# Padding tiles in SBUF so that matmul operands begin at other byte offsets, in a two-block network on one core

## The chip, the core and the metric

The kernel runs on one core of a Trainium2 chip. The metric is device time in microseconds (us) from one execution of the whole program. The profile used below was taken in one execution; other runs were timed without it.

TensorE (PE in the profile) multiplies a **stationary** operand, which a weight load (PEld) puts into the array, by a **moving** operand, which streams past it column by column. In the code `pe.matmul(ps, lhsT=..., rhs=...)` names them: `lhsT` is stationary, `rhs` is moving. The profile prints a matmul as `out<-moving,stationary`. Both operands are read from SBUF, where every tile has a byte offset that is the same in all 128 partitions.

## What is computed

The reference chains two small networks on one sequence of 256 tokens with width 1024, all in float32. Cut to what matters:

```python
# first block
a = rmsnorm(h, sb_pre_g)
q, k, v = split(a @ sb_w_qkv)
h = h + rmsnorm(merge(stick_breaking_attention(q, k, v)) @ sb_w_o, sb_post_g)
h = h + rmsnorm(conv_ffn(rmsnorm(h, ffn_pre_g[0]), ...), ffn_post_g[0])
# second layer: keys, values and forget gates from one projection, queries from another
k, v, f = split(rmsnorm(h, kv_norm_g) @ w_kvf)
q = rmsnorm(h, fox_pre_g) @ fox_w_q
h = h + rmsnorm(merge(forgetting_attention(q, k, v, cumsum(log_sigmoid(f + b_f)))) @ fox_w_o, fox_post_g)
h = h + rmsnorm(conv_ffn(rmsnorm(h, ffn_pre_g[1]), ...), ffn_post_g[1])
# second block
x = pool_layer(h, ...)      # u, z = h @ w_in; window means of u, grouped product, times silu(z), @ w_out
x = mla_layer(x, ...)       # latent q and kv, rotary part, causal softmax, times silu(z), @ w_out
return rmsnorm(x, final_norm)

def conv_ffn(x, w_up, conv_w, conv_b, w_down):      # w_up [1024, 5632], w_down [2816, 1024]
    gate, up = split(causal_depthwise_conv3(x @ w_up, conv_w) + conv_b)
    return (gelu(gate) * up) @ w_down
```

## The kernel before

**Arithmetic.** Each float32 operand is held as a high part and a low part in the type fp32r, and each product is made of three matmuls: high by high, high by low, low by high. The helper `mm3` (L70 to L72) issues them one after the other, and `mm3s` (L78, L79, L81) does it for several blocks of the contraction at once. So nearly every matmul of the program stands at one of these six lines, and it is the tile names that tell the stages apart.

**Weights.** All weights come from HBM once. The SyncE queue loads 1 MB chunks into three `raw` buffers. ScalarE (ACT) copies a part of 1024 elements per partition into a tile `wh` (L55), and VectorE (DVE) subtracts to get `wl` (L59). There are eight `wh` and eight `wl` buffers. This work is issued in between the other work of ACT and DVE by calls of `bg`.

**Two orientations of matmul.** Where the output is wanted transposed (features on partitions), the weights are stationary and the activations move: 256 columns, one for each token. This is `proj_A`, which makes `psu` (the up-projections of both FFN layers, and the input projection of the pool layer), `psq`, `psz` and `psg`. Where the output is wanted with tokens on partitions, the activations are stationary and 512 columns of weights move. This is `out_rows`, which makes `accD` (down-projection, from `gT`: tiles `gh`, `gl`), `accO` (attention outputs, from `oT` or `yT`) and `accP` (pool output, from `yT`), and `values_all`, which makes `accV`. Every matmul is preceded by a weight load of its own, of 128 columns.

**Placement.** Tiles are placed in SBUF in the order in which their pools are opened: `cst`, `rawp`, `whp`, `wlp`, `gp`, `nat`, `jk`, `sm`, `atp`, and then the pools of one stage (`sb` and `sbv`; `ff` and `fg`; `fx` and `fxv`; `pl` and `plc`; `ml` and `mlc`), which are closed at the stage's end. A tile's offset is thus the sum of what was placed ahead of it. Taken modulo 512 bytes, it comes to few values, because most tiles are multiples of 512 bytes long: in the kernel before all `wh` and `wl` buffers lie at 96, and all activations that meet weights (`aT`, `fT`, `qT`, `kT`, `ph`, `oT`, `gT`, `yT`) at 416. Steps inside these tiles (128, 256 or 512 columns of 4 bytes) are multiples of 512 bytes, but for the halves of the 192- and 320-column weight parts in the last layer, which are 256 bytes off.

**Order.** The order of instructions on each engine is the order of the code (`manual_schedule`), and semaphores are put in where tiles depend on each other.

Of the kernel before, what the change touches and what calls it, by code (L numbers as in the profile page):

```python
# [7 lines left out]
F32 = mybir.dt.float32  # L8
# [7 lines left out]
P = 128  # L16
# [11 lines left out]
TW = 1024  # L28
L3 = 384
WBUFS = 8  # L30
RAWB = 3
NLE_SET = 6

# [2 lines left out]
def tile_net(ctx: ExitStack, tc: tile.TileContext, t, out):  # L36
# [4 lines left out]
    cst = ctx.enter_context(tc.tile_pool(name="cst", bufs=1))  # L41
    rawp = ctx.enter_context(tc.tile_pool(name="rawp", bufs=RAWB))
    whp = ctx.enter_context(tc.tile_pool(name="whp", bufs=WBUFS))
    wlp = ctx.enter_context(tc.tile_pool(name="wlp", bufs=WBUFS))
    gp = ctx.enter_context(tc.tile_pool(name="gp", bufs=3))
    nat = ctx.enter_context(tc.tile_pool(name="nat", bufs=2))
    jk = ctx.enter_context(tc.tile_pool(name="jk", bufs=1))
    sm = ctx.enter_context(tc.tile_pool(name="sm", bufs=4))
    atp = ctx.enter_context(tc.tile_pool(name="atp", bufs=1))
    pacc = ctx.enter_context(tc.tile_pool(name="pacc", bufs=4, space=PSUM))  # L50
    pmm = ctx.enter_context(tc.tile_pool(name="pmm", bufs=4, space=PSUM))


    def hi_copy(hi, src, scale=1.0):
# [102 lines left out]
    def bg_hi():  # L157

        n = nxt["hi"]
        if n >= len(parts) or (n >= WBUFS and parts[n - WBUFS]["used"] < parts[n - WBUFS]["need"]):  # L160
            return False
# [11 lines left out]
    def bg_lo():  # L173
        while nxt["lo"] < nxt["hi"]:
# [4 lines left out]
            if n == specs[q["chunk"]][1][-1]:  # L179
                load_w(q["chunk"] + RAWB)  # L180

    def bg(m=1):
        for _ in range(m):
            bg_lo()
            if not bg_hi():
                break
        bg_lo()
# [116 lines left out]
    def gain(name, idx=None, g=None):  # L304
        src = t[name][idx] if idx is not None else t[name]
        n = src.shape[0]
        if g is None:
            g = gp.tile([P, D], F32, tag="g", name="g")[:, 0:n]
        nc.sync.dma_start(out=g, in_=src.unsqueeze(0).to_broadcast([P, n]))
        return g  # L310

    load_w(RAWB - 1)

# [298 lines left out]
    bg(0)  # L612
    with tc.tile_pool(name="sb", bufs=2) as sb, tc.tile_pool(name="sbv", bufs=1) as sbv:
        vv = [sbv.tile([P, NT, D], F32R, name=n) for n in ("vh", "vl")]
        oT = [sbv.tile([P, KD, S], F32R, name=n) for n in ("oTh", "oTl")]
        g_post = gain("sb_post_g", 0)
        values_all(aT, W["sb_v"], vv, {
# [101 lines left out]
    def ffn(l, aT, a1, late, dst):  # L719


        cp = conv[l]
        with tc.tile_pool(name=f"ff{l}", bufs=3) as ff, tc.tile_pool(name=f"fg{l}", bufs=1) as fg:
            gT = [fg.tile([P, NF, S], F32R, name=n) for n in ("gh", "gl")]

            def conv_gate(f, ps):
                y = ff.tile([P, 2, S], F32, tag="yc", name="yc")
                for u in range(2):
                    q = u * NF + f
                    act.activation(out=y[:, u, :], in_=ps[:, u * S:(u + 1) * S],  # L730
                                   func=AF.Identity, bias=cp[:, 132 + q:133 + q],
                                   scale=cp[:, 88 + q:89 + q])
                for u in range(2):
                    q = u * NF + f
                    for d in (1, 2):
                        w = cp[:, 88 - 44 * d + q:89 - 44 * d + q]
                        dve.scalar_tensor_tensor(out=y[:, u, d:S],  # L737
                                                 in0=ps[:, u * S:(u + 1) * S - d],
                                                 scalar=w, in1=y[:, u, d:S],
                                                 op0=ALU.mult, op1=ALU.add)  # L740
                    if u == 0:
                        act.activation(out=y[:, 0, :], in_=y[:, 0, :], func=AF.Gelu_apprx_tanh)  # L742
                bg_hi()
                dve.tensor_tensor(out=y[:, 1, :], in0=y[:, 0, :], in1=y[:, 1, :], op=ALU.mult)
                bg_lo()
                split(gT[0][:, f, :], gT[1][:, f, :], y[:, 1, :])
                bg(1)

            xs = nat_start(aT, [W["up_g", l, 0], W["up_u", l, 0]], lambda: all_T(a1, aT, 1))
            for c in range(1, NF // 2):  # L750
                wg, wu = get_w(W["up_g", l, c]), get_w(W["up_u", l, c])
                for pp in range(2):
                    f = 2 * c + pp
                    ps = mm_tile("psu")
                    proj_A(ps[:, 0:256], aT, wg, pp * P, KD)
                    proj_A(ps[:, 256:512], aT, wu, pp * P, KD)
                    conv_gate(f, ps)
                    if f == 10:
                        g_post, g = late()

            for e in range(2):
                ps = mm_tile("psn")
                nat_T(ps[:, 0:256], xs, e)
                nat_T(ps[:, 256:512], xs, e + 2)
                conv_gate(e, ps)
            acc = [acc_pair(f"accD{i}") for i in range(NT)]
            wd = {}
            for m, f in enumerate(DOWN):
                if f % 2 == 0:
                    wd[f // 2] = get_w(W["down", l, f // 2])  # L770
                for i in range(NT):
                    if m < NF - TAIL[i]:
                        out_rows(acc[i], i, gT, wd[f // 2], [(f, f % 2)], m == 0, False)
                if m < NF - TAIL[0]:
                    bg(1)
            tail = [[(f, f) for f in DOWN[NF - x:]] for x in TAIL]
            w = lambda f, c0, n: wd[f // 2](f % 2, c0, n)
            return edge(lambda: out_rows(acc[0], 0, gT, w, tail[0], False, True, by_half=True),
                        lambda: out_rows(acc[1], 1, gT, w, tail[1], False, True, by_half=True),
                        acc, lambda i, a: post_add(i, a, g_post), g, dst)  # L780


    def causal_mask(m):

        pool.memset(m, 0.0)
        pool.affine_select(out=m, in_=m, pattern=[[-1, S]], compare_op=ALU.is_ge, fill=NEG, base=P,
                           channel_multiplier=1)
# [39 lines left out]
    with tc.tile_pool(name="fxa", bufs=1) as fxa:  # L827
# [6 lines left out]
        table_set(NLE_SET)  # L834
        with tc.tile_pool(name="fx", bufs=2) as fx, tc.tile_pool(name="fxv", bufs=1) as fxv:
            vv = [fxv.tile([P, NT, D], F32R, name=n) for n in ("vh", "vl")]
            oT = [fxv.tile([P, KD, S], F32R, name=n) for n in ("oTh", "oTl")]
            bf = sm.tile([H, 1], F32, tag="bf", name="bf", bufs=1)
            nc.sync.dma_start(out=bf, in_=t["b_f"].rearrange("(h o) -> h o", o=1))
# [100 lines left out]
    with tc.tile_pool(name="pl", bufs=2) as pl_, tc.tile_pool(name="plc", bufs=1) as plc:  # L940
# [61 lines left out]
        def group(g):  # L1002
            wg = get_w(W["p_g", g])
            pT_, zs = st.pop(("pl", g)), st.pop(("zs", g))
            yT = [pl_.tile([P, 4, S], F32R, tag=n, name=n) for n in ("yh", "yl")]
            for c in range(2):
                ps = mm_tile("psg")
                for pp in range(2):
                    f = 2 * c + pp
                    proj_A(ps[:, pp * S:(pp + 1) * S], pT_, wg, f * P, 4)  # L1010
                for pp in range(2):
                    f = 2 * c + pp
                    y = zs[:, f, :]
                    q = 4 * g + f
                    dve.scalar_tensor_tensor(out=y, in0=ps[:, pp * S:(pp + 1) * S],
                                             scalar=pscale[:, q:q + 1], in1=y,
                                             op0=ALU.mult, op1=ALU.mult)
                    split(yT[0][:, f, :], yT[1][:, f, :], y)
                bg(3)
            st["y", g] = yT  # L1020
# [58 lines left out]
    with tc.tile_pool(name="ml", bufs=2) as ml, tc.tile_pool(name="mlc", bufs=1) as mlc:  # L1079
# [3 lines left out]
        gain("mla_q_norm_2", 0, gq)  # L1083
        gain("mla_kv_norm_2", 0, gkv)
        causal_mask(cmask)
        qT = [mlc.tile([P, 3, S], F32R, name=n) for n in ("qTh", "qTl")]
        kT = [mlc.tile([P, 2, S], F32R, name=n) for n in ("kTh", "kTl")]

# [127 lines left out]
        def values(g):  # L1216
            wkv = st.pop(("wkv", g))
            v = [ml.tile([P, NT, 512], F32R, tag=n, name=n, bufs=1) for n in ("vh", "vl")]
            for i in range(NT):
                psv = mm_tile("psv")  # L1220
                po = psv.rearrange("p (a b) -> p a b", a=4)
                for k in range(2):
                    r = [x.rearrange("p (a b) -> p a b", a=4)[:, :, 128:256] for x in wkv(k, 0, 1024)]
                    mm3(po, (kT[0][:, k, tok(i)], kT[1][:, k, tok(i)]), r, k == 0, k == 1)
                split(v[0][:, i, :], v[1][:, i, :], psv)
            bg(1)
            st["v", g] = v
            st["y", g] = [[ml.tile([P, 2, S], F32R, tag=f"{n}{a}", name=n, bufs=1) for n in ("yh", "yl")]
                          for a in range(2)]

# [253 lines left out]
```

## Time and profile before

| | us |
|---|---|
| three timed runs, median | 987.77 |
| lowest and highest of the three | 986.27 and 990.99 |
| the profiled execution, its own time | 987.21 |
| the profiled execution, span from first to last instruction | 985.5 |

The profile counts an engine as busy while at least one of its instructions runs. A matmul's recorded time is from its start to the end of its pass through the array, and the next one starts long before that: recorded times of 277 ns for 256 columns overlap. What a matmul costs in a dense stretch is the **step**, the time from its start to the start of the next matmul. It can be read from the starts in a timeline, or from the number of matmuls in a stretch.

### The profile page before, as it was taken

The numbers are of one execution on the slowest core, as the hardware profiler recorded it, in microseconds if no ns is written. First come the engines' busy times: TensorE is split into PE (matmuls) and PEld (weight loads), VectorE is DVE, ScalarE is ACT, GpSimd is POOL, SyncE is SP. The second block draws the span as 40 slices with busy tenths as digits, with TensorE's granted clock in tenths as the row PEclk, the third lists the DMA queues.
The fourth block names the chain that finished last, engine by engine and source line by source line (L and its number), as shares of the span: only waits on it lengthen the run. The fifth ranks groups of instructions, "written<-read, shape, count | busy, mean of one in ns | idle before, by whom it ended". The sixth has DMA issues, their size and how long they took to land.

```text
span 985.5 us, 17580 instructions
## 1 busy us (share of the span) xinstructions
PE 971.7 (99%) x6954; PEld 893.7 (91%) x6954; DVE 756.5 (77%) x1302; ACT 609.6 (62%) x1049; POOL 71.9 (7%) x181
## 2 busy tenths in 40 slices
PE   9999999999999999999999999999999999999997
PEld 6999789999887899889999988899998899999996
DVE  6577788999945979977999963776857677887776
ACT  6499866767634657657667653565434455766563
POOL 1022220000001000020000000200000020110100
PEclk9999999999999999999999999999999999999999
DMA  8733446575572754525666565375555344644421
GB/s 298 243 93 143 129 161 210 186 248 181 195 236 83 224 164 150 161 97 177 209 224 204 184 243 171 103 240 205 175 198 193 110 134 135 211 153 144 157 97 43
DMA packets 116164, 170.27 MB, mean 173 GB/s; under 512 B 4218, under 2 KB 93682, under 8 KB 116082
## 3 DMA queue, kind: packets, MB, share of 16 engines
q1 hardware_dynamic: 116002, 169.15, 52.0%
q8 instruction: 54, 0.88, 0.4%
q14 instruction: 28, 0.23, 0.1%
q0 software_dynamic: 64, 0.00, 0.0%
q10 hardware_dynamic: 16, 0.00, 0.0%
HBM read 168.10 MB, written 1.05 MB: 172 GB/s over the span
## 4 chain that ended last, share of the span: by engine, by line
PE 87%; ACT 4%; DVE 4%; POOL 1%; issue 1%; DMA 1%; POOLq 0%; DVEq 0%; ACTq 0%
PE psu L72 10%; PE psu L71 10%; PE psu L70 10%; PE accD L72 4%; PE accD L71 4%; PE accD L70 4%; PE psq L70 3%; PE psq L72 3%; PE psq L71 3%; PE accO L70 2%; PE accO L72 2%; PE accO L71 2%; DVE wl L59 2%; PE accP L70 2%; PE accP L72 2%; PE accP L71 2%
## 5 line engine op out<-in xcount | busy, mean ns | idle before, releaser
L59 DVE TENSOR_TENSOR wl<-raw,wh 128x1024 fp32r<-128x1024 f32 (+3 forms) x300 | 352.5, 1197 | 93.1 <-ACT wh L55 90.3
L55 ACT ACTIVATE wh<-raw 128x1024 fp32r<-128x1024 f32 (+3 forms) x316 | 315.3, 1026 | 83.3 <-PE accD L72 32.7
L70 PE MATMUL psu<-aT,wh 128*128 128x256 f32 x864 | 239.4, 277 | 0.6 <-ACT zs L950 0.6
L72 PE MATMUL psu<-aT,wl 128*128 128x256 f32 x864 | 239.4, 277 | 0.0
L71 PE MATMUL psu<-aT,wh 128*128 128x256 f32 x864 | 239.2, 277 | 0.0
L70 PEld LDWEIGHTS psu<-aT,wh 128*128 128x128 f32 x864 | 162.0, 188 | 0.9 <-ACT zs L950 0.8
L71 PEld LDWEIGHTS psu<-aT,wh 128*128 128x128 f32 x864 | 162.2, 188 | 0.0
L72 PEld LDWEIGHTS psu<-aT,wl 128*128 128x128 f32 x864 | 162.2, 188 | 0.0
L737 DVE SCALAR_TENSOR_TENSOR yc<-psu,conv,yc 128x255 f32<-128x255 f32 (+1 forms) x160 | 73.5, 480 | 11.2 <-ACT yc L730 8.1
L70 PE MATMUL accD<-wh,gh 128*128 128x512 f32 x176 | 69.6, 396 | 0.0
L71 PE MATMUL accD<-wl,gh 128*128 128x512 f32 x176 | 69.5, 395 | 0.0
L72 PE MATMUL accD<-wh,gl 128*128 128x512 f32 x176 | 69.5, 395 | 0.0
L337 POOL TENSOR_TENSOR ss<-ss,epsc 128x1 f32<-128x1 f32 x23 | 11.7, 507 | 616.3 <-ACT junk L374 616.2
L70 PE MATMUL psq<-aT,wh 128*128 128x256 f32 x192 | 54.1, 282 | 0.1
L72 PE MATMUL psq<-aT,wl 128*128 128x256 f32 x192 | 53.4, 278 | 0.0
L71 PE MATMUL psq<-aT,wh 128*128 128x256 f32 x192 | 53.4, 278 | 0.0
L730 ACT ACTIVATE yc<-psu,conv 128x256 f32<-128x256 f32 x80 | 40.8, 560 | 18.8 <-PE psu L72 18.7
L742 ACT ACTIVATE yc<-yc 128x256 f32<-128x256 f32 x44 | 18.4, 418 | 48.9 <-DVE yc L737 48.9
L71 PEld LDWEIGHTS accD<-wl,gh 128*128 128x128 f32 x176 | 33.0, 188 | 8.0
L72 PEld LDWEIGHTS accD<-wh,gl 128*128 128x128 f32 x176 | 33.0, 188 | 8.0
L70 PEld LDWEIGHTS accD<-wh,gh 128*128 128x128 f32 x176 | 33.0, 188 | 7.9
L55 ACT ACTIVATE qkh<-psq 128x512 fp32r<-128x512 f32 x32 | 19.0, 594 | 32.4 <-PE psq L72 32.2
(347 smaller groups left out, 2275.8 us busy)
## 6 DMA issues: line engine op xcount, KB each, us to landing
raw<-in_w_up_dram SPq DMA_DIRECT2D x44, 1024.0 KB, 5.1
raw<-in_w_down_dram SPq DMA_DIRECT2D x22, 1024.0 KB, 5.1
raw<-in_pool_w_in_dram SPq DMA_DIRECT2D x16, 1024.0 KB, 7.9
raw<-in_sb_w_qkv_dram SPq DMA_DIRECT2D x10, 1024.0 KB, 6.2
raw<-in_w_kvf_dram SPq DMA_DIRECT2D x8, 1024.0 KB, 5.8
raw<-in_pool_w_out_dram SPq DMA_DIRECT2D x8, 1024.0 KB, 5.2
raw<-in_mla_w_in_dram SPq DMA_DIRECT2D x8, 1024.0 KB, 6.0
raw<-in_mla_w_out_dram SPq DMA_DIRECT2D x8, 1024.0 KB, 6.4
```

The lines of the kernel that those rows point to most:

```text
L55: act.activation(out=hi, in_=src, func=AF.Copy, scale=scale)
L59: (eng or dve).tensor_tensor(out=lo, in0=src, in1=hi.bitcast(F32), op=ALU.subtract)
L70: pe.matmul(ps, lhsT=l[0], rhs=r[0], start=first, stop=False)
L71: pe.matmul(ps, lhsT=l[0], rhs=r[1], start=False, stop=False)
L72: pe.matmul(ps, lhsT=l[1], rhs=r[0], start=False, stop=last)
L337: pool.tensor_tensor(out=s0, in0=s0, in1=epsc[:, 0:1], op=ALU.add)
L730: act.activation(out=y[:, u, :], in_=ps[:, u * S:(u + 1) * S], func=AF.Identity, bias=cp[:, 132 + q:133 + q], scale=cp[:, 88 + q:89 + q])
L737: dve.scalar_tensor_tensor(out=y[:, u, d:S], in0=ps[:, u * S:(u + 1) * S - d], scalar=w, in1=y[:, u, d:S], op0=ALU.mult, op1=ALU.add)
L742: act.activation(out=y[:, 0, :], in_=y[:, 0, :], func=AF.Gelu_apprx_tanh)
```

## The change

A helper `pad` is added. It places a tile that nothing reads or writes. It is called for the pools `cst` (928 bytes) and `jk` (192 + 320 = 512 bytes), and in each stage ahead of the tiles that are stationary in 512-column matmuls (192 bytes), and in the last layer also ahead of `qT` and `kT` (320 bytes).

```diff
 WBUFS = 8
+APART = 320
 RAWB = 3
...
+    def pad(pl_, n, name):
+        pl_.tile([P, n // 4], F32, tag=name, name=name, bufs=1)
+
+    pad(cst, 928, "pad0")
+    pad(jk, 192 + APART, "pad1")
...
         vv = [sbv.tile([P, NT, D], F32R, name=n) for n in ("vh", "vl")]
+        pad(sbv, 512 - APART, "pad2")
         oT = [sbv.tile([P, KD, S], F32R, name=n) for n in ("oTh", "oTl")]
...
+            pad(fg, 512 - APART, "pad3")
             gT = [fg.tile([P, NF, S], F32R, name=n) for n in ("gh", "gl")]
...
             vv = [fxv.tile([P, NT, D], F32R, name=n) for n in ("vh", "vl")]
+            pad(fxv, 512 - APART, "pad4")
             oT = [fxv.tile([P, KD, S], F32R, name=n) for n in ("oTh", "oTl")]
...
+            if g == 0:
+                pad(pl_, 512 - APART, "pad5")
             yT = [pl_.tile([P, 4, S], F32R, tag=n, name=n) for n in ("yh", "yl")]
...
+        pad(mlc, APART, "pad7")
         qT = [mlc.tile([P, 3, S], F32R, name=n) for n in ("qTh", "qTl")]
...
+            if g == 0:
+                pad(ml, 512 - APART, "pad6")
             st["y", g] = [[ml.tile([P, 2, S], F32R, tag=f"{n}{a}", name=n, bufs=1) for n in ("yh", "yl")]
```

No instruction is added, removed or moved on any engine, and every wait stays. What changes is the byte offset of tiles. For the operands of the matmuls, modulo 512 bytes, as the built programs have it:

```
matmuls                                  moving            stationary
                                         before  after     before  after
psu psq psz psg   256 columns            416     320       96      0     activations past weights
accD accO accP    512 columns            96      0         416     0     weights past gT, oT, yT
accV psv          512 columns            96      0         416     320   weights past aT, kT
accS psr          256 columns            96      0         416     320   weights past aT, qT
accL              384, 320 columns       96      0         416     320   weights past aT
po (heads_out)    512, 256 columns       416     320       416     320   probabilities past values
po (last layer)   256, 128 columns       416     0         416     320   probabilities past values
z from ntri       384, 128 columns       416     320       416     0     log terms past a triangle, ones
z from qkh, qkl   256, 128 columns       416     320       416     320   keys, queries
transposes        128 columns            128     32        96, 416 0, 320
```

So in the kernel before every operand of a product of activations and weights begins 32 bytes past a multiple of 64, and afterwards at a multiple of 64. The distance from stationary to moving stays what it was, 320 or 192 modulo 512, except for `accD`, `accO`, `accP`, where it goes to 0, and for `z` from `ntri`, where it goes from 0 to 320. In the parts of the last layer that are 256 bytes off, both are shifted alike. The tiles that DVE, ACT and the DMA queues work on are shifted with them: `raw` from 96 to 0, `yc`, `us` and `zs` from 416 to 320.

## Prediction

> **What bounds the kernel now.** I first read the busy shares, the granted clock and the chain of work that ended last, on the page.
>
> ```profile
> span 985.5 us, 17580 instructions
> PE 971.7 (99%) x6954; PEld 893.7 (91%) x6954; DVE 756.5 (77%) x1302; ACT 609.6 (62%) x1049; POOL 71.9 (7%) x181
> PEclk9999999999999999999999999999999999999999
> PE 87%; ACT 4%; DVE 4%; POOL 1%; issue 1%; DMA 1%; POOLq 0%; DVEq 0%; ACTq 0%
> ```
>
> PE is busy from end to end at the full granted clock, and 87% of the chain is its matmuls. The sum is therefore one of matmul steps, and an engine that is busy 99% by overlapping records may still step more slowly than it could. So I read steps next, from four stretches in which one kind of matmul runs without a wait.
>
> ```profile
> core 0: us, PE busy (x) PEld busy (x) DVE busy (x) ACT busy (x) POOL busy (x), PEclk, DMA share, GB/s
> 150.00:250.00 100.00, 100.00 (x885) 100.00 (x884) 90.52 (x149) 69.77 (x112) 0.00 (x0) 1.00 0.63 206
> 460.00:558.00 98.00, 98.00 (x868) 98.00 (x867) 89.01 (x145) 68.29 (x111) 0.00 (x0) 1.00 0.61 201
> 682.00:698.00 16.00, 16.00 (x138) 16.00 (x137) 11.57 (x16) 6.35 (x8) 0.00 (x0) 1.00 0.70 230
> 262.00:312.00 50.00, 50.00 (x216) 40.29 (x215) 26.20 (x28) 21.72 (x29) 2.02 (x7) 1.00 0.56 190
> ```
>
> A count holds the matmuls that started in the stretch and some two that were already running. The first stretch is `psu` of the first FFN: 100 us by 883 is **113.3 ns** a step for 256 columns, and the second FFN gives the same (98 by 866). The third is `psu` of the pool layer: 16 us by 136 is **117.7 ns**, for the same tiles at the same offsets. The fourth is `accD`: 50 us by 214 is **233.6 ns** for 512 columns. Short matmuls come from the timeline of the first attention, PE alone.
>
> ```profile
> 52.45 0.33 PE L682 MATMUL z<-nl,ntri 128*128 128x384 f32 x1
> 52.62 0.22 PE L685 MATMUL z<-nh,nones 128*128 128x128 f32 x1
> 52.68 0.27 PE L685 MATMUL z<-nl,nones 128*128 128x128 f32 x1
> 52.79 0.39 PE L682 MATMUL z<-nh,ntri 128*128 128x384 f32 x1
> ```
>
> The 128 columns that start at 52.62 take a step of 60 ns (52.62 to 52.68). The next step, 110 ns, is longer because its successor's weights are loaded only after its own. Transposes, also 128 columns, go at that pace too, as the chain of waits shows (0.87 by 8 is 109 ns).
>
> ```profile
> 251.27 0.87 PE psn L467 x8
> ```
>
> So 109 ns is what one weight load costs, whatever streams. From 128 to 256 columns the step grows by 53.3 ns, 0.417 ns a column. Taken back to no columns, 6.7 ns are left, the time of 16 columns, and 16 columns of 4 bytes are **64 bytes**. Every operand begins 32 bytes past a multiple of 64. A stream read in pieces of 64 bytes would touch 17 of them for 256 columns in place of 16, and 17 by 6.67 is 113.3. That is my reason to expect something of the new offsets. It is a fit to two points, and no row has an aligned stream to compare with.
>
> At 512 columns the same reckoning gives 33 by 6.67, 220 ns, so 13.6 ns of the 233.6 are something else. One part of it may be the distance between the operands. The trace has 512-column matmuls with both operands at one residue (416): `po` in the two attentions.
>
> ```profile
> L70 PE MATMUL po<-ph,vh 128*128 128x512 f32 x16 | 6.3, 397 | 0.0
> L71 PE MATMUL po<-pl,vh 128*128 128x512 f32 x16 | 6.4, 402 | 0.3 <-DVE pl L59 0.3
> L72 PE MATMUL po<-ph,vl 128*128 128x512 f32 x16 | 6.3, 393 | 0.0
> L70 PE MATMUL accD<-wh,gh 128*128 128x512 f32 x176 | 69.6, 396 | 0.0
> L71 PE MATMUL accD<-wl,gh 128*128 128x512 f32 x176 | 69.5, 395 | 0.0
> L72 PE MATMUL accD<-wh,gl 128*128 128x512 f32 x176 | 69.5, 395 | 0.0
> ```
>
> Their recorded times average 397 ns against 395 of `accD`, which is 320 apart. A distance of 0 by itself, at an offset of 32 past 64, gains nothing here.
>
> **The change part by part.** Nothing is removed, added or moved, and every wait stays. `pad` issues no instruction. So the terms are changes of a step, times counts.
>
> *Streams of 256 columns.* The counts, from the groups by shape (in each the lines 70, 71 and 72 have equal counts, 78, 79 and 81 likewise):
>
> ```profile
> L70 PE MATMUL psu<-aT,wh 128*128 128x256 f32 x864 | 239.4, 277 | 0.6 <-ACT zs L950 0.6
> L70 PE MATMUL psq<-aT,wh 128*128 128x256 f32 x192 | 54.1, 282 | 0.1
> L70 PE MATMUL psq<-fTh,wh 128*128 128x256 f32 x64 | 18.5, 288 | 0.0
> L70 PE MATMUL psq<-qTh,wh 128*128 128x256 f32 x48 | 13.4, 279 | 0.0
> L70 PE MATMUL psq<-kTh,wh 128*128 128x256 f32 x32 | 8.9, 277 | 0.0
> L70 PE MATMUL psz<-aT,wh 128*128 128x256 f32 x128 | 36.2, 283 | 0.0
> L70 PE MATMUL psg<-ph,wh 128*128 128x256 f32 x64 | 17.9, 279 | 0.0
> L78 PE MATMUL accS<-wh,aT 128*128 128x256 f32 x96 | 23.7, 284 | 0.6 <-ACT aT L55 0.5
> ```
>
> Three times 1,488 is 4,464 matmuls. The distance between their operands stays, and both go to multiples of 64. The stream alone would fall from 113.3 to 106.7, but the weight load holds the step at 109 to 111 (the transposes and the 110 above). I take 110, a gain of 3.3 ns each, also for those that now go at 117.7, whose further 4.4 ns I leave in place: **14.7 us**. The bounds are a gain of 8.7 (117.7 to 109) and a loss of 4.4 (113.3 to 117.7), since the trace shows both steps at one offset and a new offset could settle on either.
>
> *Streams of 512 columns.*
>
> ```profile
> L78 PE MATMUL accV<-wh,aT 128*128 128x512 f32 x64 | 25.9, 405 | 0.8 <-ACT aT L55 0.7
> L70 PE MATMUL accO<-wh,oTh 128*128 128x512 f32 x64 | 26.1, 407 | 0.0
> L70 PE MATMUL accP<-wh,yh 128*128 128x512 f32 x64 | 25.3, 396 | 0.0
> L70 PE MATMUL accO<-wh,yh 128*128 128x512 f32 x56 | 22.5, 402 | 0.0
> L70 PE MATMUL psv<-wh,kTh 128*128 128x512 f32 x16 | 6.8, 425 | 0.7 <-DVE qkl L59 0.6
> ```
>
> With `accD` and `po` that is three times 456, or 1,368. One piece of 64 bytes less is 6.7 ns off 233.6: **9.1 us**. The bounds are 20 ns (to 213.3, which is 512 columns at 0.417) and a loss of 5. That loss is the spread of the six rows of `po` and `accD` around their mean, 393 to 402. Setting the distance of `accD`, `accO` and `accP` to 0 I count at nothing, by the `po` rows.
>
> *The rest.* Transposes, `z` and the short products are 600-odd matmuls held by weight loads or by waits: nothing. DVE, ACT and DMA also get new offsets. I count that at nothing, because PE covers it: in the first stretch DVE is busy for 90.5 of 100 us, and with PE's step at 110 the same work would have 97. If their instructions became 7% longer, that cover would be gone. The DMAs take 0.63 of their engines' time there.
>
> *What is given back.* Where PE waits for weights, a faster PE waits longer. The chain has such places at the start of the pool layer and in the last layer.
>
> ```profile
> 636.86 8.02 DMA raw<-in_pool_w_in_dram
> 816.42 3.37 DVE wl L59 x2
> 846.98 4.85 DMA raw<-in_mla_w_out_dram
> ```
>
> I put some 85 us there (636 to 660 and 800 to 860) under weights instead of PE, 9% of the span, and take 9% off: 23.8 becomes **21.7 us**. The profiled execution took 987.2 us in all, 1.7 more than its span and 0.6 below the median of the runs, so both give the same: 987.2 less 21.7 is **965.5 us**.
>
> **What the skill says against it.** The Trainium skill, in the page "SBUF — State Buffer" under "Specifications (TRN2)", gives SBUF lines of 16 bytes. All offsets here, before and after, are multiples of 16. By that rule no stream touches a line more or less, and the time stays; that is the second rival below. The skill's page "TensorE: Matmul & The Clock Gate", under "Back-to-back issue gap", puts a step at the columns over 2.4 GHz plus 2.5 ns, which is 109.2 and 215.8 ns. The trace is above both, by 4 to 8 and by 18 ns. If that whole difference came from placement, the sum would be near that of the first rival. No row shows that it does.
>
> **The rivals.** *All of the excess goes.* The excess of 512 columns (20 ns over 213.3) is three times that of 256 (6.7), so it grows with the stream, as a cost for each piece read would. If alignment takes all of it, 512 columns gain 18 ns (24.6 us), and 256 columns gain 4.3, or 8.7 where they step 117.7 (I take a third of them): 26 us. Less 9%, the time is 941. Against it: at one set of offsets the pool layer steps 117.7 and the FFN 113.3, so part of the excess has nothing to do with offsets.
>
> *Nothing.* Pieces smaller than 64 bytes, or reads far ahead of their use, would make the 6.7 ns a fixed cost of each matmul. Two points on a line can't exclude it, and the `po` rows show no effect of distance. The time is then 987, with 2 us to either side from the spread of the timed runs.
>
> *Only the 512-column streams gain.* If the weight load and its stream disturb each other by their distance, only `accD`, `accO` and `accP` change: three times 360, or 1,080 matmuls, by 8 to 18 ns, 9 to 19 us. The time is then 969 to 979. The `po` rows speak against it, though they lie off a multiple of 64.
>
> *Slower.* The two steps at one offset look like two ways in which load and stream can fall in with each other. If with the new offsets the FFN falls into the slow one, its 1,920 `psu` and an estimated 1,000 of the others take 4.4 ns more: 12.8 us, and the time is 1000. It decides if the 512 columns gain less than 9 ns at the same time. For it speaks that equal distances gave 113.3 in one stage and 117.7 in another. Against it, the FFNs hold 113.3 through 960 matmuls twice.
>
> **How the numbers follow.** The forecast (one piece of 64 bytes less, 955 to 975) has 0.39, only 512 columns 0.16, all of the excess 0.13, nothing 0.20, slower 0.12. The predicted time is the forecast's, 965.5. A range from 940 to 992 takes in the forecast, the 512 columns alone, nothing, and half of the first rival, and leaves out 0.19. A measurement of this kernel can tell about 0.5% from no change, which is 982.8 to 992.7. Faster holds the first three, 0.68, the same 0.20, slower 0.12.
>
> **What would show it.** In the profile after, the FFN stretches would have some 910 matmuls in 100 us where 885 stand, and `accD` 222 in 50 us where 216 stand. If `accD` has 233, the whole excess went. If `psu` stays at 885 and `accD` rises, it was the distance. If the step of 128 columns before a loaded successor stays at 60 ns though aligned, the 16 columns were never a piece of 64 bytes and my reason falls. If the FFN shows 852, it is the slow mode. A busier DVE in the FFN with PE waiting on `wl` would show that the cover I counted on is gone.

## The result, and the profile after

| | before, us | after, us |
|---|---|---|
| timed runs, median (7 of each, on one chip) | 987.77 | 981.51 |
| lowest to highest | 986.0 to 992.37 | 980.02 to 982.5 |
| profiled execution, its own time | 987.21 | 981.37 |
| profiled execution, span | 985.5 | 979.7 |

The ratio after to before is 0.9926, with an interval of 0.9903 to 0.995. (The ratios here and below are estimated from all timed runs and can differ a little from those of the medians.) The kernel became faster by 6 us, where the prediction had 22 us. The busy shares and the chain, from the page of the changed kernel:

```profile
span 979.7 us, 17580 instructions
PE 965.0 (99%) x6954; PEld 893.3 (91%) x6954; DVE 756.7 (77%) x1302; ACT 609.7 (62%) x1049; POOL 71.9 (7%) x181
PE 88%; ACT 5%; DVE 3%; POOL 2%; issue 1%; DMA 1%; SPq 0%; POOLq 0%; DVEq 0%; ACTq 0%
```

The other engines work as long as before. PE is busy for 6.7 us less, and it is still the bound. The four stretches of the prediction, in the changed kernel (stretch, then busy time and count for each engine):

```profile
150.00:250.00 100.00, 100.00 (x885) 100.00 (x884) 90.37 (x148) 70.11 (x112) 0.00 (x0) 1.00 0.61 204
460.00:558.00 98.00, 98.00 (x867) 98.00 (x866) 89.51 (x146) 67.82 (x109) 0.00 (x0) 1.00 0.59 194
682.00:698.00 16.00, 16.00 (x138) 16.00 (x138) 12.22 (x15) 8.07 (x10) 0.00 (x0) 1.00 0.59 199
262.00:312.00 50.00, 50.00 (x224) 41.42 (x223) 27.09 (x29) 21.89 (x30) 2.02 (x7) 1.00 0.56 189
```

`psu` has 885 matmuls in 100 us, as before, although both of its operands now begin at a multiple of 64 bytes. Only `accD` moved, from 216 to 224 in 50 us, of which two are owed to shorter steps at the end of the stretch: `accD` ends there at 311.6 us, and transposes follow. The starts in the trace give its settled step as 226.7 ns in place of 233.3. Summed over all their matmuls, waits between them included, the steps fell by 3.5 us for `accD`, 0.8 for `accO` and 1.2 for `accP`. Together these 5.4 us (before rounding) are nearly all of the 5.8 by which the profiled time fell; the steps of everything else together changed by 0.4. `accV`, whose operands stay 192 apart, kept its 233.3 ns. One more distance changed than the section on the change says: `po` of the last layer, 96 short matmuls, went from 0 to 192. Its steps sum to 10.6 us before and after.

The groups of `accD` and `po` in the changed kernel (recorded time of one matmul behind the comma):

```profile
L79 PE MATMUL accD<-wh,gh 128*128 128x512 f32 x176 | 68.7, 390 | 0.0
L80 PE MATMUL accD<-wl,gh 128*128 128x512 f32 x176 | 68.5, 389 | 0.0
...
L80 PE MATMUL po<-pl,vh 128*128 128x512 f32 x16 | 6.5, 408 | 0.3 <-DVE pl L68 0.3
L81 PE MATMUL po<-ph,vl 128*128 128x512 f32 x16 | 6.3, 395 | 0.0
L79 PE MATMUL po<-ph,vh 128*128 128x512 f32 x16 | 6.3, 394 | 0.0
```

`accD` went from 395 to 390 at distance 0. `po` has distance 0 before and after, and it stands at 399. So the prediction's comparison of these two was not one of distance. The timeline shows a likely reason: PE at the beginning of a run of `accD`, and 13 us into it (start, recorded time):

```profile
251.62 0.47 PE L79 MATMUL accD<-wh,gh 128*128 128x512 f32 x1
251.93 0.39 PE L80 MATMUL accD<-wl,gh 128*128 128x512 f32 x1
252.16 0.39 PE L81 MATMUL accD<-wh,gl 128*128 128x512 f32 x1
252.39 0.40 PE L79 MATMUL accD<-wh,gh 128*128 128x512 f32 x1
252.62 0.39 PE L80 MATMUL accD<-wl,gh 128*128 128x512 f32 x1
252.85 0.40 PE L81 MATMUL accD<-wh,gl 128*128 128x512 f32 x1
253.08 0.39 PE L79 MATMUL accD<-wh,gh 128*128 128x512 f32 x1
...
264.42 0.39 PE L81 MATMUL accD<-wh,gl 128*128 128x512 f32 x1
264.65 0.39 PE L79 MATMUL accD<-wh,gh 128*128 128x512 f32 x1
264.87 0.39 PE L80 MATMUL accD<-wl,gh 128*128 128x512 f32 x1
```

The first step is 310 ns and the next five 230 each (251.93 to 253.08, 1.15 us). Later the same timeline shows two steps in 0.45 us (264.42 to 264.87); by the finer starts of the trace they are 226 and 227 ns. In the starts of all runs of `accD`, `accO` and `accP` it takes mostly between three and ten matmuls until the short step is reached, and a run of `po` is over after three.

### The profile page after: what moved, and what is told of

Its sections match the earlier page's. It is cut to its first block, busy times and chain, and to the rows that moved or that the text cites. A ratio compares the mean times of both kernels' runs of the same rounds, so it can differ in the third digit from the quotient of the medians.

```text
span 979.7 us, 17580 instructions
## 1 busy us (share of the span) xinstructions
PE 965.0 (99%) x6954; PEld 893.3 (91%) x6954; DVE 756.7 (77%) x1302; ACT 609.7 (62%) x1049; POOL 71.9 (7%) x181
## 4 chain that ended last, share of the span: by engine, by line
PE 88%; ACT 5%; DVE 3%; POOL 2%; issue 1%; DMA 1%; SPq 0%; POOLq 0%; DVEq 0%; ACTq 0%
PE psu L79 10%; PE psu L80 10%; PE psu L81 10%; PE accD L81 4%; PE accD L80 4%; PE accD L79 4%; PE psq L79 3%; PE psq L81 3%; PE psq L80 3%; PE accO L79 2%; PE accO L81 2%; PE accO L80 2%; PE accP L79 1%; PE accP L81 1%; PE accP L80 1%; DVE wl L68 1%
```

## The experiments

The theories were: the gain is one of **distance** between the two operands of a matmul; of **alignment** to 64 bytes; or of the **other engines'** access to SBUF, whose tiles moved too. A later question was what sets the two steps of 256-column matmuls, 113.3 and 117.7 ns.

**Alignment alone (e1) and distance alone (e2).** The change has two kinds of padding, which can be had apart. e1 keeps the two that move whole pools to multiples of 64 and leaves out those of the stages, so that every distance between a matmul's operands is as in the kernel before. e2 is the reverse.

```diff
 e1, against the changed kernel
-        pad(sbv, 512 - APART, "pad2")
-            pad(fg, 512 - APART, "pad3")
-            pad(fxv, 512 - APART, "pad4")
-                pad(pl_, 512 - APART, "pad5")
-        pad(mlc, APART, "pad7")
-                pad(ml, 512 - APART, "pad6")
 e2, against the changed kernel
-    pad(cst, 928, "pad0")
-    pad(jk, 192 + APART, "pad1")
```

> The change with its two first pads alone (928 bytes in cst, 512 in jk), so that every operand goes from 32 past a multiple of 64 to a multiple of 64 and no distance between stationary and moving operand changes. If the distance is all that counts (A), steps stay at 113.3 and 117.7 ns for 256 columns and at 233.4 for 512, and the time is that of before, 987.8 within 2 us. If a multiple of 64 is what made the 512-column steps shorter (B, the reason of the prediction), accD goes to 227 and the time to about 981.5.

> The change without its two first pads: weights stay at 96 and the streamed inputs at 416 modulo 512, and gT, oT and yT go from 416 to 96, so that the 512-column matmuls of accD, accO and accP have distance 0 while every operand still begins 32 past a multiple of 64. By A accD steps 227 ns and the time is that of the change, 981.5 within 1.5 us. By B accD stays at 233.4 and the time is 987.8.

e1 took 986.08 us (median of 12) beside 987.04 of before on the same chip, a ratio of 0.9997 (0.9981 to 1.0012). e2 took 981.73 (12 runs), a ratio of 0.996 (0.994 to 0.998). Its median is that of the change; two of its runs, 986.61 and 990.34, bring the ratio nearer to 1. The stretches of the first FFN's `psu` and of `accD` in e1:

```profile
150.00:250.00 100.00, 100.00 (x885) 100.00 (x884) 90.36 (x148) 70.17 (x112) 0.00 (x0) 1.00 0.61 203
262.00:312.00 50.00, 50.00 (x216) 40.09 (x215) 26.19 (x28) 21.72 (x29) 2.06 (x7) 1.00 0.55 189
```

Here everything is aligned, and both counts are those of the kernel before. The short matmuls of the first attention, in the timeline of e1, answer the test that the prediction set for its 64 bytes:

```profile
52.21 0.22 PE L694 MATMUL z<-nh,nones 128*128 128x128 f32 x1
52.27 0.27 PE L694 MATMUL z<-nl,nones 128*128 128x128 f32 x1
```

The step of 128 columns is 60 ns (52.21 to 52.27) with both operands aligned, as it was 32 bytes off. In e2, where operands again lie 32 bytes past a multiple of 64, the same two stretches are:

```profile
150.00:250.00 100.00, 100.00 (x885) 100.00 (x884) 90.46 (x149) 69.72 (x112) 0.00 (x0) 1.00 0.62 206
262.00:312.00 50.00, 50.00 (x222) 41.33 (x222) 27.51 (x30) 21.71 (x29) 2.03 (x7) 1.00 0.56 190
```

The `accD` starts give 226.7 ns, the step of the changed kernel. So the distance makes the gain, and alignment gives nothing that these runs can tell.

**Every distance (e3).** A kernel of PE work alone: after one load from HBM, runs of 36 matmuls, each run at one distance from stationary to moving operand, 0 to 480 bytes in steps of 32, for 512 and for 256 columns. Further runs put both operands at another residue, split the moving operand in two parts, or take 384 columns. In the code `run` takes the columns and the residues of the moving and the stationary operand, and `gap` makes four transposes. The network is left out. Two of the further runs stand for all in the cut.

```diff
+    for x in range(16):
+        gap()
+        run("F" + L[x], 512, 32 * x, 0)
+    for x in range(16):
+        gap()
+        run("H" + L[x], 256, 32 * x, 0)
...
+    gap(); run("Kfive", 512, 320, 320)
+    gap(); run("Kthree", 512, 96, 416)
...
```

> None of the reference is computed: rows of 36 matmuls alone on PE, a row for each distance from the stationary to the moving operand in steps of 32 bytes (0 to 480 modulo 512), once with 512 and once with 256 columns, stationary at 0; then a few rows with both operands at 32 and at 320, with the moving operand in two parts of 256 columns, with 384 columns, and rows of 256 columns straight behind rows of 512. By A the 512-column step depends on the distance alone: about 227 ns at 0, 233.4 at 192, the same with both at 32 or 320; the 256-column step is 113.3 or 117.7 at 320 and about 119.7 at 0. If other engines' reads and writes of SBUF make the excess (C), the steps here, with DVE, ACT and DMA idle, are near 213 and 109 at every distance. If the way a row is entered sets 113.3 or 117.7 (D), the rows of 256 columns at 320 differ with what ran ahead of them.

Some runs in the timeline of e3 (start, time of the whole run; `Fc`, `Fe`, `Fg`, `Fi` are 512 columns at 64, 128, 192 and 256, `Kfive` at 0 with both at 320, `Kthree` at 192 with both off 0):

```profile
28.85 8.50 PE L56 MATMUL Fc<-mov,sta 128*128 128x512 f32 x36
46.40 8.61 PE L56 MATMUL Fe<-mov,sta 128*128 128x512 f32 x36
64.06 8.65 PE L56 MATMUL Fg<-mov,sta 128*128 128x512 f32 x36
81.73 8.47 PE L56 MATMUL Fi<-mov,sta 128*128 128x512 f32 x36
...
236.09 8.43 PE L56 MATMUL Kfive<-mov,sta 128*128 128x512 f32 x36
244.72 8.65 PE L56 MATMUL Kthree<-mov,sta 128*128 128x512 f32 x36
```

36 matmuls take 8.43 to 8.47 us at 0 and 256, and 8.65 at 192, wherever the pair lies. The mean steps, from the starts of the 13th to the 36th matmul of each run:

```
distance mod 512   512 columns   256 columns
0, 256             226.7         120.0
64, 320            228.8         117.8
128, 384           232.8         118.8
192, 448           233.3         117.8
the odd 32s        233.3-234.6   117.8-120.1
```

The very first run, at 0, gives 227.6: after the first, six of its steps are 427 ns, and it settles late. The pattern repeats after 256 bytes. DVE, ACT and POOL did nothing in these stretches and the DMA queues moved next to nothing, and 226.7 and 233.3 ns stand there as in the kernel, so the other engines are not the cause of the difference. A moving operand in two parts keeps the steps, 226.7 at 0 and 233.2 at 192. Two further readings: 384 columns take 173.3 ns at 0 and at 192 alike, so of the two widths only 512 columns lose at 192; and 0, the best for 512 columns, is among the worst for 256. The short step of 256 columns, 113.3, does not occur in e3 at all, not even in the two runs straight behind 512 columns that were meant to bring it about.

**The other distance that `APART` allows (e4), and none (e5).** The constant sets the distance of the activations that meet weights. With 192, `psu`, `psq`, `psz`, `psg` go from 320 to 192, and `accV` from 192 to 320. With 0 every pair goes to distance 0.

```diff
 e4
-APART = 320
+APART = 192
 e5
-APART = 320
+APART = 0
-        pad(mlc, APART, "pad7")
```

> The change with APART at 192 in place of 320: aT, fT, qT, kT and ph lie at 192 modulo 512, weights and gT, oT, yT at 0 as in the change. 256-column streams then have distance 192 (was 320), accV, psv and accL 320 (was 192). The sweep had 512 columns at 228.9 ns for 320 and 233.3 for 192, so accV and psv should gain 4.4 ns on 240 matmuls, 1.0 us. If 192 makes the 256-column streams fall into the 113.3 ns step more often than 320 does (E: accS, at 192, came to 113 within five matmuls after nearly every wait), psq, psz and the pool layer's psu go from 117.7 to 113.3 and the time falls by up to 9 us, to 973. If 192 and 320 are alike for them (F, as in the sweep, 117.8 at both), the time is 980 to 981.

> The change with APART at 0: every operand at 0 modulo 512, so that the distance is 0 in all products. By A, with the steps of the sweep, 4,464 streams of 256 columns step 119.8 ns in place of 115.2 on the mean (20.5 us more), and accV and psv fall from 233.3 to 227 (1.5 us less): some 1000 us. By B, where a common residue at a multiple of 512 would be best for all, the time is at or under 981.5.

e5 took 999.76 us (4 runs, 999.71 to 999.93), a ratio of 1.0102 (1.007 to 1.0134). Both FFN stretches and `accD` in e5:

```profile
150.00:250.00 100.00, 100.00 (x836) 100.00 (x835) 85.10 (x140) 65.03 (x104) 0.00 (x0) 1.00 0.59 196
460.00:558.00 98.00, 98.00 (x819) 98.00 (x818) 83.28 (x135) 64.01 (x102) 0.00 (x0) 1.00 0.59 198
262.00:312.00 50.00, 50.00 (x223) 41.39 (x222) 30.06 (x34) 23.79 (x30) 0.19 (x1) 1.00 0.61 211
```

Taking the two matmuls already running off the count, `psu` steps 120 ns (100 us by 834), and its 2,592 matmuls cost 14.3 us more than in the changed kernel, while the settled step of `accV` falls from 233.3 to 227.0. This is the largest effect of the study, and the sweep's table has its sign and size.

e4 took 980.58 us (6 runs, 978.35 to 983.73), a ratio of 0.9909 (0.9883 to 0.9936). It can't be told from the changed kernel. As the table has it for distance 320, `accV` settles at 228.9. The table has one figure for 256 columns at 320 and 192, but the kernel has not. The two FFN stretches in e4:

```profile
150.00:250.00 100.00, 100.00 (x851) 100.00 (x851) 86.60 (x140) 67.36 (x108) 0.00 (x0) 1.00 0.57 191
460.00:558.00 98.00, 98.00 (x867) 98.00 (x867) 88.58 (x144) 67.93 (x110) 0.00 (x0) 1.00 0.60 202
```

The first FFN takes the long step, 117.7 ns, through 960 matmuls, and the second the short one, at the same offsets in one execution. The difference is 960 by 4.4, or 4.2 us. In the same profile the steps of `psq` sum to 1.9 us less than in the changed kernel, and the execution profiled was the slowest of the six.

**What decides between the two steps (e6, e7).** PE alone again. e6 begins runs of 24 matmuls of 256 columns in four ways: behind transposes (T), behind transposes and a wait for ACT of 0.7 us (W), behind eight matmuls of 512 columns at 192 (V), and behind fifteen at 0 (Y). e7 puts odd matmuls ahead of runs of 20, at distances 64 and 192.

```diff
 e6
+        run("T" + L[x], 256, 32 * x, 0, 24)
+        act.activation(out=sta[:, 0:512], in_=gap(), func=AF.Copy)
+        run("W" + L[x], 256, 32 * x, 0, 24)
...
 e7
+    KICKS = [None, (128, 0, 1), (128, 0, 2), (64, 0, 1), (384, 0, 1), (320, 0, 1), (192, 0, 1),
+             (256, 1, 1), (256, 1, 3), (512, 0, 1), (512, 128, 2)]
```

> None of the reference is computed: rows of 24 matmuls of 256 columns at distances 0 to 224 in steps of 32 bytes, each entered in four ways: T straight behind four transposes, W behind a wait for ACT, which writes the stationary operand anew, V behind 8 matmuls of 512 columns at distance 192, Y behind 15 of 512 columns at distance 0. If the entry decides between 113.3 and 117.7 (D), rows of one distance differ by T, W, V and Y, and W and V reach 113.3 at 192. If it is only the distance, all four rows of a distance agree with the sweep (117.8 to 120) and the 113.3 of the FFN has another cause, such as the work of other engines.

> None of the reference is computed: rows of 20 matmuls of 256 columns at distances 64 (which is 320 less 256) and 192, entered behind transposes (T), behind 512 columns at distance 0 (Y) or behind 512 columns at 192 or 64 (U). Ahead of each row stands nothing, or one to three odd matmuls: 128, 64, 384, 320, 192 or 512 columns, or 256 columns at distance 0. If the 113.3 and 117.7 ns are two ways in which the weight loads and the streams can stand to each other, kept from one matmul to the next (D), then an odd matmul ahead of a row moves it from 117.7 to 113.3 in some of the eleven cases, and the same one does so at every entry or not depending on where it leaves the two. If the step was fixed by the engine's history of waits, no odd matmul changes it and all rows entered by T or Y stay at 117.7.

Four runs of e6 in its timeline (`c` is distance 64, `g` 192):

```profile
50.13 3.08 PE L51 MATMUL Tc<-mov,sta 128*128 128x256 f32 x24
54.39 2.99 PE L51 MATMUL Wc<-mov,sta 128*128 128x256 f32 x24 [0.75 <-ACT sta L59]
...
127.95 3.08 PE L51 MATMUL Tg<-mov,sta 128*128 128x256 f32 x24
...
137.37 2.90 PE L51 MATMUL Vg<-mov,sta 128*128 128x256 f32 x24
```

At 64 the starts give 117.8, 113.4, 117.8, 117.8 ns for T, W, V, Y; at 192 they give 117.7, 113.4, 113.4, 117.7; at 0 it is 120.0 in all four, and at the distances in between every entry gave one of 116.6 to 120.4. The 113.3 appears at 64 and 192 alone, and there it depends on what came ahead of the run.

e7 has three entries: transposes (T), twelve matmuls of 512 columns at 0 (Y), and six of 512 at 64 or 192 (U). At 64, of 33 runs 29 stayed at 117.8 and three went to 113.3; the first can't be read, since the program begins with steps of 213. At 192 the runs without an odd matmul have 113.3 behind T and 117.8 behind Y and U. There a single matmul of 192, 320 or 512 columns, or two of 128, moved the run to 113.3 behind Y and U, and behind T it kept the 113.3. Others, such as one of 64 columns, moved it from 113.3 to 117.8 behind T. Of three runs at 192, the one behind T without an odd matmul, and those behind Y without one and with one of 192 columns, the timeline has:

```profile
155.49 2.53 PE L54 MATMUL Tqa<-mov,sta 128*128 128x256 f32 x20
...
190.54 2.52 PE L54 MATMUL Yqa<-mov,sta 128*128 128x256 f32 x20
...
224.41 2.47 PE L54 MATMUL Yqg<-mov,sta 128*128 128x256 f32 x20
```

The whole time of the first holds a step of 206 ns at its beginning; from the third on, its steps are 113 and 114. In e6 the same entry at the same distance, `Tg`, gave 117.7. So the four transposes right ahead of a run don't settle its step; what further back does was not found.

**Two attempts to use it (e8, e9).** e8 gives `aT` 128 bytes of room, so that modulo 256 it lies at 64 (as 320 does) in the FFNs and at 192 elsewhere. It also leaves out the pad of 928 bytes, so weights and activations lie 32 past a multiple of 64 again. e9 is e4 with seven odd matmuls of 192 columns, each ahead of a long run; their results are overwritten by the matmul behind them.

```diff
 e8, against the changed kernel
-APART = 320
+APART = 192
-    pad(cst, 928, "pad0")
...
+            a = atp.tile([P, KD // 2 * S + 32], F32R, tag=f"aT{'hl'[k % 2]}{k // 2}", name="aT")
+            o = 32 * ((k + far) % 2)
...
 e9, against e4
+            l, r = w(k, c0, m), at(aT, k, ALL)
+            if odd and k == 0:
+                pe.matmul(ps[:, 0:192], lhsT=l[0], rhs=r[0][:, 0:192], start=True, stop=True)
...
```

> A version meant to beat both: the distances are chosen by stage. gT, oT, yT stay at distance 0 from the weights. aT gets 128 bytes of room, so that it lies at distance 320 in the two FFNs (where psu was at 113.3 ns in both profiles) and at 192 in the attentions, the pool layer and the last layer (where e4 had psq and psz at 113.3 for most rows). By D, with the rows entered as in e4 and in the change, psq gains 1.9 us, psz 0.4, accV and psv 0.7 on the change: 978 to 979, and up to 974 if the pool layer's psu falls into 113.3 as well. If FFN rows at 320 come in at 117.7 here, as they did at 192 in e4, 4.3 us are lost for each and the gain is gone.

> The kernel of e4 (all stationary operands that meet aT at distance 192) with 7 additional matmuls of 192 columns, each ahead of a long run of 256-column matmuls at distance 192: the first psq of the second block, the first psu of each FFN, three places of the pool and the last group's psg. Their results are overwritten by the matmul that follows. Theory D (at distance 192 a run keeps the step it starts with, and an odd matmul ahead of it starts it in the short one, as rows c, f, g of e7 did): psu of both FFNs at 113.3 ns, psz and psg mostly so, span of the profile and median 974 to 976 us, and the 4.3 us between the timed runs of e4 (one FFN in the long step) gone: all runs within 1.5 us. Rival (in the kernel the waits inside a run decide, not its beginning): median 980 to 981 us, the spread of e4 kept, and one FFN's psu at 117.7 in about half of the runs.

e8 took 979.37 us (6 runs: three from 976.91 to 977.54, three from 981.2 to 983.84), a ratio of 0.9926 (0.9902 to 0.9951). In its profile, an execution of 977.12, the two FFNs and the pool layer show:

```profile
150.00:250.00 100.00, 100.00 (x885) 100.00 (x884) 90.60 (x149) 70.44 (x112) 0.00 (x0) 1.00 0.62 204
460.00:558.00 98.00, 98.00 (x860) 97.70 (x859) 90.32 (x148) 67.62 (x109) 0.00 (x0) 1.00 0.61 200
682.00:698.00 16.00, 16.00 (x141) 15.91 (x140) 13.48 (x19) 7.43 (x11) 0.00 (x0) 1.00 0.61 191
```

Both FFNs have the short step there: the second ends at 555 us, inside its stretch, and its starts give 113.3. So has most of the pool layer (141 in place of 138, in a stretch that outlasts the short run). One timed run of e8, 976.91, is the lowest single time of the study, but the median can't be told from that of the change. e9 took 980.85 us (6 runs, 979.37 to 981.88), a ratio of 0.99 (0.9885 to 0.9914), and its profile has:

```profile
150.00:250.00 100.00, 100.00 (x885) 100.00 (x884) 90.14 (x148) 70.06 (x112) 0.00 (x0) 1.00 0.62 203
460.00:558.00 98.00, 98.00 (x835) 98.00 (x834) 85.97 (x140) 64.66 (x105) 0.00 (x0) 1.00 0.58 191
682.00:698.00 16.00, 16.00 (x143) 16.00 (x142) 11.99 (x16) 7.01 (x10) 0.00 (x0) 1.00 0.71 230
```

Five of the seven runs began in the short step, among them the first FFN and the pool layer. The second FFN kept the long one, with the same odd matmul ahead of it. So the theory's 974 to 976 was not reached. That a run keeps its step through 960 matmuls held in each profile; that one odd matmul sets it does not hold in the kernel, where the matmuls ahead of it differ. What in them decides stays open. The two groups of e8's timed runs lie 5 us apart on the mean, a little more than one FFN in the other step, but timed runs have no trace, so that this is their cause is only argued.

## Why the prediction was wrong

- **PE as the bound, and steps as the unit of the sum**: right. The change is one of steps, and the chain and the busy times of the other engines stayed.
- **The 64 bytes**: this is the main step that failed. It read the 6.7 ns left over at no columns as one more piece of 64 bytes for operands 32 bytes off, and made of it 14.7 us for 256 columns and 9.1 us for 512. With alignment alone e1 gave nothing: 885 and 216 matmuls, 60 ns for 128 columns. The prediction called this a fit to two points; the same two points allow a fixed cost, its second rival, and that holds for alignment.
- **Distance counted at nothing, by the `po` rows**: wrong. e2 has the gain from it, 3.5 us in `accD` alone. The rows could hardly show it, because a run of three ends before the step has settled. The comparison also used recorded times, where a settled run differs by 5 ns in 395.
- **The size for 512 columns**: 6.7 ns by the wrong reason, and 6.7 ns in the settled `accD`; that they agree is luck, and so is that the time fell at all, since what the prediction counted on gave nothing and what it counted at nothing gave the gain. And the 6.7 ns hold for the 1,080 matmuls of 512 columns whose distance went to 0, not for all 1,368, and for the settled ones alone: `accD` gave 3.5 of a possible 3.5 us, `accP` 1.2 of 1.3, `accO`, with its shorter runs and its waits, 0.8 of 2.4.
- **256 columns**: nothing in place of 14.7 us. The last layer's 256-column `accO`, 47 steps at distance 0, went from 113.6 to 119.7 and lost 0.3 us.
- **Given back**: 9% was set aside for stretches that wait for weights. The steps sum to 5.4 and the profile to 5.8, so no loss there can be seen.
- **The rivals**: what happened is the third, only the 512-column streams, at 0.16, with 6.7 ns where it took 8 to 18, so that its 969 to 979 us were not reached either. The prediction's test for it, `psu` at 885 and `accD` risen, is what the profile shows. The slower case's mechanism exists: e4 has an FFN in the 117.7 step. It took 4.2 us there, for one FFN. The change kept the distance of both at 320, and in its profile both have 113.3.
- **The skill's rule**: the Trainium skill's lines of 16 bytes (page "SBUF — State Buffer", "Specifications (TRN2)") gave no change from alignment, and e1 agrees, at 0.9997. It says nothing of a distance, and the time did change. The Trainium skill's page "TensorE: Matmul & The Clock Gate", under "Step-by-step: what each phase is for", has two independent read ports, so that loading the next weights takes nothing from the running matmul. In e3, with nothing else running, the step was 226.7 or 233.3 by where the stationary operand lay relative to the moving one, so in their timing the two are not independent here. What they share no run shows. The formula that the prediction took from the same page of the Trainium skill, under "Back-to-back issue gap", is given there for an isolated matmul, and not for a stream of loads and matmuls. The estimates from it, 109.2 and 215.8 ns, were not reached here, where the settled steps are 113.3 and 226.7 at best.

## What to carry to other kernels

Look at the distance between the stationary and the moving operand modulo 256 bytes, not at their alignment: in this kernel dense 512-column matmuls in fp32r with a weight load each ran best at 0, and 256-column ones badly there, so each stage wants its own. Whether another type or a kernel without a weight load for each matmul has this was not tested. Before a row is taken as evidence for a rate, see how long its runs are and how many matmuls the rate needs to settle. A step that differs between two stages at equal offsets is a sign that the history of the engine counts, and then one profile of a small change can mislead by several us.

## What had not been expected of the hardware

At distances 0, 64 and 192 the settled steps lie on a grid of 6.67 ns, the time of 16 columns at 0.417 ns: 113.3 is 17 units, 120.0 is 18, 173.3 is 26, 226.7 is 34 and 233.3 is 35, and the mixed ones are thirds (117.78 is 17 and two thirds, 228.9 is 34 and a third). At other distances they don't: 232.8, 234.6 and 116.6 are in between. Nor do single steps (117, 118, 118), only their means. So the 16 columns that the prediction read as bytes come back as a time, but what has this period was not tested, nor whether the effect goes away when a weight load is left out.

At distance 0 all 256-column runs settle at one step, 120.0, and the timed runs of e5 lie within 0.22 us of each other, where those of the kernel before lie 6 us apart. The most uniform placement was the slowest of those that were tried.
